# Background sums of the modulation: another set of rates at which weight tiles bring them along

## The chip, the cores and the metric

One core of one Trainium2 chip. The metric is the device time of one execution in microseconds, as the median of three runs. The engines are named as the profile names them: PE is TensorE, DVE VectorE, ACT ScalarE, POOL GpSimd, SP SyncE (which here issues the DMAs).

## The reference

A generator of two layers over 256 context tokens and 256 latent tokens, width 2048. Each layer modulates a normalised input with shift, scale and gate, which are products of a conditioning vector with a 2048 x 6144 matrix, then runs two attention groups and an output projection:

```
for l in range(DEPTH):                       # DEPTH = 2
    shift, scale, gate = split(silu(c) @ w_ada[l] + b_ada[l], 3)
    shift_c, scale_c, gate_c = split(silu(c_ctx) @ w_ada[l] + b_ada[l], 3)
    h_lat = rms_norm(x, norm_g[l]) * (1 + scale) + shift
    h_ctx = rms_norm(xc, norm_g[l]) * (1 + scale_c) + shift_c
    lat_a, lat_b = mixer_inputs(h_lat, w_in[l], ...)   # q, k, v, gate of GQA; low-rank q, kv, gate of latent attention
    ctx_a, ctx_b = mixer_inputs(h_ctx, w_in[l], ...)
    o_a = block_attention(GQA: latent queries over context and latent keys)
    o_b = block_attention(latent attention, likewise)
    x = x + gate * (concat(o_a * silu(g_gqa), o_b * silu(g_mla)) @ w_out[l])
    if l < DEPTH - 1:
        xc = xc + gate_c * (the same for the context tokens)
return rms_norm(x, final_g)
```

Scale and shift of layer 0 are wanted at once; the gates of layer 0 are wanted at its output projection, scale and shift of layer 1 at the start of layer 1, and the gate of layer 1 at its end.

## The kernel before

**Main work.** Every projection runs over weight tiles of 512 KB (288 KB where 288 columns remain). `wtile` (line 107) loads one on SP into one of four `raw` buffers, ACT rounds it to `hi` (line 116), and DVE, or POOL for every fifth tile, writes the remainder `lo` in two halves (line 118); `lo` has two buffers. `mm3` then makes each product of three matmuls (lines 143 to 145: hi by hi, lo by hi, hi by lo). In layer 0 a first part (until about 178 us) makes the first modulation and the first half of the input projection; then come the kv, q and gate projections with the two GQA head groups in between (`gqa_heads`, scores at line 605), the two low-rank projections `cq` and `ckv`, the four pairs of latent heads (`mla_qr`, line 691 for its rotary transposes, `mla_pair`, `mla_heads`), and the output projection in four column blocks c = 0 to 3 with residual update `go` and `xn` (lines 823 and 825). Layer 1 does the same for latent tokens alone, and its output projection is spread over its four head pairs.

**Background work.** What of the modulation is not wanted at once is computed on DVE beside this main work, by a generator `ada_rest` (line 308). One step of it (one turn of `ada_half`, line 263) loads one 512 KB piece of the transposed modulation matrix (`rad`, on SP, two buffers, issued behind the `raw` load before it) and multiplies it with the broadcast conditioning vectors `cb`, summing along the row: two sums of 512 elements for each vector (line 286, the output called `junk`, the sum `as`). The profile lists every sum as two DVE records, the sum itself and a short accumulator read. There are 128 steps: 96 with two vectors, so four sums each (gates of layer 0, then scale and shift of layer 1), and after these 32 with one vector, two sums each (gate of layer 1); 448 sums in all. `ada_done` stores each finished piece (`mod` tiles, `gate_d`).

**What sets when steps come.** Each weight tile adds the present rate to a debt, and takes one step for each whole unit of it:

```
self.bg_due += self.bg_rate
while self.bg and self.bg_due >= 1.0 and not self.hold:
    self.bg_due -= 1.0
    self.bg_step()
```

The rate is BG0 from line 937 on (the GQA part, the low-rank projections and their gates: 56 weight tiles), BG1 from line 972 on (latent attention of layer 0: 14 tiles), BG3 from line 997 on (output projection, c = 0 to 2: 24 tiles), then zero, and BG2 from line 1054 on in layer 1 (64 tiles). Behind c = 2 whatever of layer 1's scale and shift is missing is done at once (line 1013); in layer 1 what is still left after the first head pair is flushed (line 1105). The sums and their loads are put in with a lower priority (line 285, offset 1500), and a scheduler that simulates the timeline makes each engine's final order; so a step need not stand where its weight tile stands. Engines work in the order that results, each one strictly in turn.

Of the kernel before, what the change touches and what calls it, by code (L numbers as in the profile page):

```python
# [39 lines left out]

BG_LATER = 1500

BGS, BG0, BG1, BG3, BG2 = 5.0, 1.3, 1.1, 0.5, 0.4
TCKW = {"schedule_with_timeline_sim": True}


# [1168 lines left out]
```

## Time and profile before

| | us |
|---|---|
| median of three runs | 1396.11 (1395.94 to 1397.76) |
| the profiled execution | 1396.79 |
| its span, first to last instruction | 1395.0 |
| PE busy | 1326.7 (95%) |
| DVE busy | 1083.2 (78%) |
| ACT busy | 580.4 (42%) |
| POOL busy | 401.0 (29%) |
| mean granted clock of PE | 0.988 |

Stages by their start in the trace, in us: first part 0; kv and GQA of layer 0 178; the low-rank projections about 392; latent attention 462; output projection 692; layer 1 about 880; its latent attention about 1190.

Busy time counts records of instructions. A matmul's end is modelled, so a stall of PE is read from the list of waits and from the share of a stretch that PE is busy. In the windows an x counts records, and for line 286 two records are one sum.

### The profile page before, as it was taken

What the parts mean: (1) busy time and instruction counts of PE and PEld (TensorE: products, weight loads), DVE (VectorE), ACT (ScalarE), POOL (GpSimd) and SP (SyncE); (2) the same over time, 40 slices, a digit from 0 to 9 for tenths busy, and PEclk for the clock granted to TensorE, in tenths of its full rate; (3) what the DMA queues carried; (4) which work ended last, traced back from release to release, by engine and by line L of the source; (5) the groups of instructions that cost most, each with busy time, mean ns of one, the idle gap of its engine ahead of it and who ended that gap; (6) DMA issues with size and microseconds to landing.
All of it is one profiled execution on the core that took longest, in us unless ns stands there. A gap on an engine that the chain in (4) does not pass through costs nothing.

```text
span 1395.0 us, 20993 instructions
## 1 busy us (share of the span) xinstructions
PE 1326.7 (95%) x7516; PEld 1125.6 (81%) x7516; DVE 1083.2 (78%) x2297; ACT 580.4 (42%) x961; POOL 401.0 (29%) x385
## 2 busy tenths in 40 slices
PE   6999998998998999899999999999999999999996
PEld 5776786877887988788887888899888889889884
DVE  3776589999999989999985536976797676857566
ACT  4322213435342233354632224664554544454443
POOL 0110014523222230222222214442344231313335
PEclk9999999998999999999999999999999999999998
DMA  9997854554556666444475446565865647633444
GB/s 307 331 321 267 301 161 135 166 173 147 179 159 204 200 220 197 157 139 141 168 241 181 148 130 201 176 195 165 272 211 182 199 155 245 239 122 114 158 144 144
DMA packets 141128, 268.31 MB, mean 192 GB/s; under 512 B 8304, under 2 KB 53856, under 8 KB 139616
## 3 DMA queue, kind: packets, MB, share of 16 engines
q1 hardware_dynamic: 141024, 266.97, 59.4%
q8 instruction: 59, 0.97, 0.3%
q14 instruction: 45, 0.37, 0.1%
HBM read 260.61 MB, written 6.33 MB: 191 GB/s over the span
## 4 chain that ended last, share of the span: by engine, by line
PE 50%; DVE 28%; DMA 12%; issue 6%; ACT 2%; POOL 1%; SPq 1%; DVEq 0%; POOLq 0%; ACTq 0%
PE acc L143 14%; PE acc L145 14%; PE acc L144 14%; DVE junk L286 11%; DMA rad<-in_w_adaT 9%; DVE lo L118 7%; PE att L605 3%; PE att L240 2%; DVE sm L610 1%; PE att L628 1%; DMA raw<-in_w_in 1%; DMA ra<-in_w_ada 1%; DVE pt L150 1%; ACT hi L116 1%; DVE cb L466 1%
## 5 line engine op out<-in xcount | busy, mean ns | idle before, releaser
L116 ACT CAST hi<-raw 128x1024 fp32r<-128x1024 f32 (+2 forms) x279 | 272.2, 977 | 410.9 <-PE acc L144 202.0
L118 DVE TENSOR_TENSOR lo<-raw,hi 128x512 fp32r<-128x512 f32 (+2 forms) x446 | 306.1, 728 | 101.8 <-PE acc L145 42.1
L118 POOL TENSOR_TENSOR lo<-raw,hi 128x512 fp32r<-128x512 f32 (+2 forms) x112 | 151.1, 1369 | 469.6 <-PE acc L145 273.7
L143 PE MATMUL acc<-hi,h 128*128 128x512 f32 (+1 forms) x672 | 238.4, 359 | 10.2 <-DVE g L466 3.0
L144 PE MATMUL acc<-hi,h 128*128 128x512 f32 (+1 forms) x672 | 238.0, 357 | 0.0
L145 PE MATMUL acc<-lo,h 128*128 128x512 f32 (+1 forms) x672 | 225.5, 359 | 2.1 <-DVE lo L118 1.8
L286 DVE CUSTOM_DVE_ANT_0 junk<-rad,cb 128x512 bf16<-128x512 f32 x224 | 172.4, 770 | 68.1 <-DMA rad<-in_w_adaT 66.1
L286 DVE CUSTOM_DVE_ANT_0 junk<-rad,cb,as 128x512 bf16<-128x512 f32 x224 | 193.1, 862 | 3.3
L144 PE MATMUL acc<-h,lo 128*128 128x512 f32 (+1 forms) x512 | 170.9, 340 | 4.4 <-DVE lo L118 4.4
L145 PE MATMUL acc<-h,hi 128*128 128x512 f32 (+1 forms) x512 | 169.9, 338 | 0.0
L143 PE MATMUL acc<-h,hi 128*128 128x512 f32 (+1 forms) x512 | 163.7, 341 | 1.8 <-ACT hi L116 1.4
L616 POOL TENSOR_SCALAR p<-p,sm 128x512 f32<-128x512 f32 (+1 forms) x96 | 85.8, 899 | 270.2 <-DVE sm L614 226.0
L143 PEld LDWEIGHTS acc<-hi,h 128*128 128x128 f32 x672 | 126.6, 189 | 33.1 <-issue 11.5
L144 PE MATMUL acc<-hi,y 128*128 128x512 f32 x384 | 149.8, 391 | 0.2 <-DVE y L150 0.2
L143 PE MATMUL acc<-hi,y 128*128 128x512 f32 x384 | 149.0, 393 | 0.7 <-ACT y L149 0.7
L145 PE MATMUL acc<-lo,y 128*128 128x512 f32 x384 | 143.8, 394 | 3.0 <-DVE lo L118 2.0
L145 PEld LDWEIGHTS acc<-lo,h 128*128 128x128 f32 x672 | 124.5, 189 | 21.7 <-DVE lo L118 2.9
L144 PEld LDWEIGHTS acc<-hi,h 128*128 128x128 f32 x672 | 127.0, 189 | 15.8
L144 PEld LDWEIGHTS acc<-h,lo 128*128 128x128 f32 x512 | 96.8, 189 | 15.4 <-DVE lo L118 5.8
L143 PEld LDWEIGHTS acc<-h,hi 128*128 128x128 f32 x512 | 93.5, 190 | 14.7 <-issue 2.5
L145 PEld LDWEIGHTS acc<-h,hi 128*128 128x128 f32 x512 | 96.7, 190 | 9.7
L145 PEld LDWEIGHTS acc<-lo,y 128*128 128x128 f32 x384 | 72.0, 188 | 20.0 <-DVE lo L118 4.6
(218 smaller groups left out, 2253.5 us busy)
## 6 DMA issues: line engine op xcount, KB each, us to landing
rad<-in_w_adaT SPq DMA_DIRECT2D x128, 512.0 KB, 4.4
raw<-in_w_in SPq DMA_DIRECT2D x125, 512.0 KB, 4.4
raw<-in_w_out SPq DMA_DIRECT2D x72, 512.0 KB, 4.1
ra<-in_w_ada SPq DMA_DIRECT2D x32, 1024.0 KB, 9.1
raw<-in_w_in SPq DMA_DIRECT2D x48, 288.0 KB, 3.0
raw<-in_w_ukv SPq DMA_DIRECT2D x16, 512.0 KB, 3.6
raw<-in_w_uq SPq DMA_DIRECT2D x12, 512.0 KB, 3.7
xT<-in_xT SPq DMA_DIRECT2D x8, 512.0 KB, 7.6
```

The costliest lines, as they stand in the source:

```text
L116: nc.scalar.copy(h, t)
L118: e.tensor_tensor(out=lo[:, c], in0=t[:, c], in1=fr(h[:, c]), op=ALU.subtract)
L143: mm(out, lhsT=ah, rhs=bh, start=first, stop=False)
L144: mm(out, lhsT=al, rhs=bh, start=False, stop=False)
L145: return mm(out, lhsT=ah, rhs=bl, start=False, stop=last)
L150: self.nc.vector.tensor_tensor(out=lo, in0=src, in1=fr(hi), op=ALU.subtract)
L240: nc.tensor.matmul(ps[32 * g : 32 * g + 32, :], lhsT=self.scp[:, m + i, o : o + 32], rhs=rs[kind, m][:, i, :], start=run is runs[0] and j ...
L286: nc.vector.tensor_tensor_reduce(out=junk, in0=r[:, cs], in1=cb[:, v, cs], scale=1.0, scalar=o if i else 0.0, op0=ALU.mult, op1=ALU.add, a ...
L466: nc.vector.tensor_tensor(out=o, in0=ps, in1=o, op=ALU.add)
L605: self.order = nc.tensor.matmul(banks[j], lhsT=q[:, qs], rhs=k[:, ks], start=i == 0, stop=i == len(score) - 1)
L610: nc.vector.tensor_reduce(out=nb[:, c], in_=v, axis=AX.X, op=ALU.max)
L616: nc.gpsimd.tensor_scalar(out=pr[j], in0=pr[j], scalar1=l[:, j : j + 1], scalar2=1.0, op0=ALU.mult, op1=ALU.mult)
```

## The change

One line of numbers:

```
-BGS, BG0, BG1, BG3, BG2 = 5.0, 1.3, 1.1, 0.5, 0.4
+BGS, BG0, BG1, BG3, BG2 = 5.0, 1.0, 1.0, 1.5, 0.4
```

In the order of the code this is 56 steps instead of 72 or 73 at BG0, 14 instead of 15 at BG1, and 36 instead of 12 at BG3; 22 instead of 28 are left for layer 1. No instruction of the main work is added or taken away.

The order of DVE in layer 0's output projection, early in column block c = 1 (before: 763 to 779 us). `lo` is the remainder of a weight tile, `junk` and `as` a background sum; a row of `as` alone is the accumulator read; `mod` is a finished scale of layer 1. Before:

```order
L118 TENSOR_TENSOR lo_7492<-raw_7489,hi_7491 128x512 x2
L295 TENSOR_TENSOR as_4354<-as_4354,as_4355 128x32
L208 TENSOR_TENSOR mod_91<-as_4354,vec_90 128x32
L118 TENSOR_TENSOR lo_7533<-raw_7530,hi_7532 128x512 x2
L286 ISA junk_7679,as_7675<-rad_7677,cb_1649 128x512
L286 ISA as_7675 128x1
L286 ISA junk_7681,as_7675<-rad_7677,cb_1649,as_7675 128x512
L286 ISA as_7675 128x1
L118 TENSOR_TENSOR lo_7564<-raw_7561,hi_7563 128x512 x2
```

The same weight tiles after the change (`lo_7493` and `lo_7534` are the tiles that were `lo_7492` and `lo_7533`):

```order
L118 TENSOR_TENSOR lo_7493<-raw_7490,hi_7492 128x512 x2
L286 ISA junk_7503,as_4814<-rad_7497,cb_1649 128x512
L286 ISA as_4814 128x1
L286 ISA junk_7505,as_4814<-rad_7497,cb_1649,as_4814 128x512
L286 ISA as_4814 128x1
L286 ISA junk_7540,as_4814<-rad_7538,cb_1649 128x512
L286 ISA as_4814 128x1
L286 ISA junk_7542,as_4814<-rad_7538,cb_1649,as_4814 128x512
L286 ISA as_4814 128x1
L286 ISA junk_7544,as_4814<-rad_7538,cb_1649 128x512
L286 ISA as_4814 128x1
L118 TENSOR_TENSOR lo_7534<-raw_7531,hi_7533 128x512 x2
```

Where no sum or two stood between the remainders of two weight tiles, five or six stand now, and the finished scale comes some 25 us of the old time later.

The order of SP's loads in the same projection, column block c = 0 going over into c = 1. `raw` is a weight tile of the output projection, `rad` a piece of the modulation matrix. Before:

```order
L98 DMA rad_7352<-in_w_adaT 128x1024
L98 DMA raw_7386<-in_w_out 128x2x512
L98 DMA raw_7417<-in_w_out 128x2x512
L98 DMA rad_7424<-in_w_adaT 128x1024
L98 DMA raw_7458<-in_w_out 128x2x512
L98 DMA raw_7489<-in_w_out 128x2x512
L98 DMA rad_7496<-in_w_adaT 128x1024
```

After:

```order
L98 DMA rad_7262<-in_w_adaT 128x1024
L98 DMA raw_7306<-in_w_out 128x2x512
L98 DMA raw_7347<-in_w_out 128x2x512
L98 DMA rad_7272<-in_w_adaT 128x1024
L98 DMA raw_7398<-in_w_out 128x2x512
L98 DMA rad_7313<-in_w_adaT 128x1024
L98 DMA rad_7354<-in_w_adaT 128x1024
L98 DMA raw_7439<-in_w_out 128x2x512
L98 DMA rad_7364<-in_w_adaT 128x1024
```

One `rad` for two `raw` has become three for two, and a `raw` can now stand behind a `rad` that waits for its buffer.

The order of DVE in layer 1, when its latent attention begins (before: 1199 to 1206 us). `qr` is the rotated query part of latent attention, `kn` the keys of the first pair of heads. Before:

```order
L118 TENSOR_TENSOR lo_11965<-raw_11962,hi_11964 128x512 x2
L286 ISA junk_12285,as_7676<-rad_12283,cb_2829 128x512
L286 ISA as_7676 128x1
L694 TENSOR_TENSOR qr_11782<-att_11836,qr_11782 64x4x128
L286 ISA junk_12287,as_7676<-rad_12283,cb_2829,as_7676 128x512
L286 ISA as_7676 128x1
L150 TENSOR_TENSOR kn_11879<-acc_11889,kn_11879 128x512
L150 TENSOR_TENSOR kn_11879<-acc_11904,kn_11879 128x512
```

After:

```order
L118 TENSOR_TENSOR lo_11997<-raw_11994,hi_11996 128x512 x2
L694 TENSOR_TENSOR qr_11818<-att_11874,qr_11818 64x4x128
L150 TENSOR_TENSOR kn_11917<-acc_11927,kn_11917 128x512
L150 TENSOR_TENSOR kn_11917<-acc_11942,kn_11917 128x512
L694 TENSOR_TENSOR qr_11818<-att_11883,qr_11818 64x4x128
```

The sums that stood ahead of `qr` and `kn` are gone from this stretch.

Counted over the whole program, the sums stand so, by the old time of the main work around them (in us; the two orders were laid side by side by the instructions of the main work, which are the same):

| stretch | 250-305 | 305-332 | 332-346 | 346-430 | 430-462 | 462-600 | 600-700 | 700-745 | 745-825 | 825-1187 | 1187-1230 |
|---|---|---|---|---|---|---|---|---|---|---|---|
| sums before | 36 | 21 | 8 | 67 | 29 | 97 | 58 | 24 | 16 | 46 | 10 |
| sums after | 32 | 20 | 0 | 44 | 24 | 97 | 56 | 31 | 64 | 44 | 0 |

Within 430 to 462, between the `lo` that DVE wrote at 432 us and the next one that it wrote, at 444.5 us, stood twelve sums; eight stand there now.

## Rows read from the trace of the kernel before

**Rows 1.** Page: busy time and share by engine; then the chain that ended last.

```profile
PE 1326.7 (95%) x7516; PEld 1125.6 (81%) x7516; DVE 1083.2 (78%) x2297; ACT 580.4 (42%) x961; POOL 401.0 (29%) x385
...
PE 50%; DVE 28%; DMA 12%; issue 6%; ACT 2%; POOL 1%; SPq 1%; DVEq 0%; POOLq 0%; ACTq 0%
```

**Rows 2.** Page, groups: busy us, mean ns of one | idle before, releaser.

```profile
L286 DVE CUSTOM_DVE_ANT_0 junk<-rad,cb 128x512 bf16<-128x512 f32 x224 | 172.4, 770 | 68.1 <-DMA rad<-in_w_adaT 66.1
L286 DVE CUSTOM_DVE_ANT_0 junk<-rad,cb,as 128x512 bf16<-128x512 f32 x224 | 193.1, 862 | 3.3
```

**Rows 3.** Windows: length, PE, PEld, DVE, ACT, POOL busy (records), clock, DMA share, GB/s.

```profile
250.00:305.00 55.00, 55.00 (x282) 46.56 (x281) 54.72 (x127) 22.32 (x41) 22.28 (x19) 1.00 0.58 182
305.00:332.00 27.00, 19.22 (x102) 16.07 (x102) 26.61 (x74) 10.29 (x23) 11.25 (x16) 0.83 0.48 146
...
430.00:446.00 16.00, 14.06 (x63) 11.30 (x61) 14.71 (x35) 1.35 (x2) 3.18 (x2) 1.00 0.50 154
446.00:462.00 16.00, 12.50 (x90) 11.53 (x91) 15.86 (x36) 8.03 (x18) 10.92 (x12) 1.00 0.53 171
462.00:600.00 138.00, 130.48 (x748) 114.74 (x746) 127.99 (x306) 47.55 (x77) 28.73 (x28) 0.99 0.62 195
...
700.00:745.00 45.00, 43.67 (x223) 36.25 (x222) 35.48 (x87) 14.21 (x23) 9.81 (x9) 1.00 0.66 228
745.00:825.00 80.00, 80.00 (x354) 66.17 (x354) 35.07 (x66) 21.38 (x31) 18.37 (x14) 1.00 0.49 158
...
1187.00:1212.00 25.00, 22.31 (x128) 19.63 (x128) 23.20 (x38) 10.55 (x16) 9.62 (x6) 0.93 0.83 291
```

**Rows 4.** Windows of line 286 alone: length, DVE busy (records), clock, DMA share, GB/s.

```profile
745.00:825.00 80.00, 12.80 (x32) 1.00 0.49 158
825.00:1100.00 275.00, 28.48 (x56) 1.00 0.64 198
...
1187.00:1212.00 25.00, 9.08 (x16) 0.93 0.83 291
```

**Rows 5.** Waits of PE, 305 to 332: total us, times, longest.

```profile
PE att L145 <- DVE pt L150: 1.9, 2, 1.0
...
PE att L143 <- DVE g L636: 1.6, 1, 1.6
```

**Rows 6.** Waits of PE, 446 to 462.

```profile
PE acc L143 <- DVE cq L470: 2.8, 1, 2.8
PE att L535 <- POOL cq L566: 2.5, 3, 1.1
```

**Rows 7.** Chain of waits, 436 to 448: start us, us, what.

```profile
440.94 3.71 DMA rad<-in_w_adaT
```

**Rows 8.** Waits of PE, 1187 to 1212.

```profile
PE att L691 <- POOL tw L676: 1.0, 1, 1.0
PE acc L143 <- DVE kn L150: 1.0, 1, 1.0
PE att L605 <- ACT qr L693: 0.7, 1, 0.7
```

**Rows 9.** Chain of waits, 1196 to 1212.

```profile
1206.82 0.12 PE acc L144
...
1207.09 0.21 PE acc L143
...
1210.07 0.21 PE acc L145
```

**Rows 10.** Waits of DVE, 745 to 825.

```profile
DVE junk L286 <- DMA rad<-in_w_adaT: 19.4, 6, 5.6
DVE lo L118 <- PE acc L145: 12.1, 5, 4.3
```

**Rows 11.** Lines of DVE, 745 to 825: busy us, mean ns | idle before, releasers.

```profile
L118 DVE TENSOR_TENSOR lo<-raw,hi 128x512 fp32r<-128x512 f32 x24 | 17.1, 755 | 21.3 <-PE acc L145 12.1 <-issue 9.2
L823 DVE TENSOR_TENSOR go<-acc,gt 128x512 f32<-128x512 f32 x8 | 5.4, 686 | 3.0 <-ACT junk L332 1.4 <-POOL xn L825 1.4 <-PE acc L145 0.2
```

## The prediction

> **What bounds the kernel now.** I began with the busy shares and the chain that ended last [rows 1]. PE is busy for 1326.7 of 1395.0 us, so at most some 68 us are open to any reordering; yet the chain goes over DVE for 28% of the span and over DMA for 12%, which says that in some stretches PE follows DVE. The two groups of line 286 [rows 2] are the work that the change moves: 448 sums, (172.4 + 193.1) / 448 = 0.82 us each, and ahead of them DVE stood idle for 66.1 us until a `rad` landed. Then I read the windows stage by stage [rows 3] and asked in each which engine is short:
>
> - 250 to 305: DVE 54.72 of 55 us, PE 55.00. Both full, nothing lost.
> - 305 to 332, the end of the first GQA group: DVE 26.61 of 27, PE only 19.22, clock 0.83. PE is 7.8 us short and DVE is what it follows.
> - 430 to 462, the change from the query to the key and value low-rank projection: PE 14.06 of 16 and 12.50 of 16, 5.4 us short, DVE again nearly full.
> - 462 to 600: DVE 127.99 of 138, PE 130.48.
> - 700 to 825, output projection: PE 43.67 of 45 and 80.00 of 80; DVE 35.48 and 35.07.
> - 1187 to 1212, start of latent attention in layer 1: DVE 23.20 of 25, PE 22.31, clock 0.93.
>
> So the output projection is where PE is the bound and DVE has 44.9 of 80 us free, and the three other places are those where sums stand ahead of what PE waits for. That is the ground on which the change moves sums from the one kind of place to the other.
>
> **The change part by part.** The sums stay 448, with the same 128 loads; what counts is where they stand, by the table under the change. Each moved step takes its `rad` load along. The terms are against the profiled execution, 1396.79 us.
>
> *End of the first GQA group, 250 to 332.* Five sums fewer (4 + 1), 5 x 0.82 = 4.1 us of DVE work. Of the 7.8 us that PE lacks, 1.9 and 1.6 are waits for DVE itself, for the probabilities `pt` and the attention output `g` [rows 5]; the rest goes over ACT and POOL, or over the lower clock. In the new order one sum still stands between nearly every two DVE instructions of this stretch (21 become 20), so the waits stay mostly as they are, and only the backlog that DVE brings along shrinks. The eight sums at 332 to 346 go as well, and PE loses nothing there now. Ends 0 and -7.8; I take -2.0, about half of the 4.1, nearer to zero, since the order at the stall itself hardly changes.
>
> *346 to 430.* 23 sums fewer, but the list of waits has none of PE here: 0.
>
> *Low-rank projections, 430 to 462.* PE waits 2.8 us for the eviction of `cq` and then three times, 2.5 in all, for POOL on the same `cq` [rows 6]. On DVE, twelve sums stand ahead of the `lo` of 444.5 us, and the one right before it waited 3.71 us for its `rad` [rows 7]; with it `lo` and the eviction behind it waited. Now eight stand there: four fewer are 3.3 us at 0.82, more than the 2.8. The POOL waits are a chain behind the eviction and stay. Ends 0 and -5.3; I take -2.5, the greater part of the first wait.
>
> *462 to 700.* 97 sums stay 97 and 58 become 56: the debt that the old rates had run up was worked off before, and the scheduler fills this stretch up again. 0. So the relief is confined to the front, about 41 sums by 475 us.
>
> *Output projection, 700 to 745.* Seven sums more, 5.7 us at 0.82, onto a DVE that is busy 35.48 of 45 us [rows 3]. It has room, but PE loses 1.3 us here already. Ends 0 and +3; I take +0.5.
>
> *Output projection, 745 to 825.* PE does 354 matmuls here [rows 3], 24 for a weight tile, so 14.75 tiles, one in 5.4 us. DVE now carries 64 sums instead of 16. Their price here is 12.80 / 16 = 0.80 [rows 4], so 51.2; `lo` and `go` add 17.1 + 5.4 [rows 11]: 73.7 of 80 us, 92%. That still fits, but it is no longer free: before, DVE waited up to 4.3 us for PE to free a `lo` buffer, 12.1 us in five waits [rows 10], and that margin is what the sums now eat. Five or six sums between two `lo` take 4.0 to 4.8 us, with 1.4 for `lo` itself 5.4 to 6.2, against 5.4. POOL takes every fifth `lo`, which gives the time back. Loads: the rate adds one step for a tile, about 15 loads of 0.52 MB, 98 GB/s on top of 158, so 256, under the 291 GB/s that one stretch moved [rows 3]. They must land in turn with two buffers, and a `rad` was what DVE waited for here even before, 19.4 us in six waits, at no cost to PE [rows 10]. A wait for a `rad` would now hold `lo` behind it on DVE and a `raw` behind it on SP, and PE waits for both. Ends 0 and +8 (next part); I take +1.5, near zero, because a density of the same kind in 250 to 305 left PE at 55.00 of 55 [rows 3].
>
> The price of a sum is not the same everywhere: 28.48 / 28 = 1.02 us in 825 to 1100 and 9.08 / 8 = 1.14 in 1187 to 1212, against 0.80 in the output projection [rows 4]. POOL is busy 9.62 of 25 us in the dear stretch, 18.37 of 80 in the cheap one [rows 3]. The Trainium skill, page "SBUF — State Buffer", section "Who interferes with whom", speaks against the change with that: a DVE instruction with two inputs in SBUF contends with a GpSimd instruction that reads SBUF, since its second input comes through a shared port that is locked exclusively. The rows agree in direction. By it all work put beside the residual update of POOL would run at the dearer price, which is the second rival below.
>
> *Layer 1, 1187 to 1230.* The ten sums here go altogether, 8 x 1.14 = 9.1 us of DVE in the first 25 us. PE waits three times, 1.0 + 1.0 + 0.7 = 2.7 us [rows 8], for `tw`, `kn` and `qr`; sums stand directly ahead of `qr` and `kn`. Behind these waits the matmuls of 256 columns follow one another 0.21 us apart instead of 0.12 for 15 matmuls [rows 9]: the granted clock is at its lower level, 1.4 us more. Without the sums `kn` and `qr` come earlier and that stretch probably stays at the full clock. The wait for `tw` is on POOL and may stay. Ends 0 and -4.1; I take -3.0. The flush behind the first head pair has nothing left to do.
>
> Sum: -2.0 - 2.5 + 0.5 + 1.5 - 3.0 = -5.5, so 1391.3 for the profiled execution. The median of before lies 0.7 under its profiled one, so 1390.6.
>
> **Rivals.**
>
> *Nothing measurable.* The waits named have other ends than the sums: PE waits for ACT and POOL in chains that are as long without them, the scheduler keeps 97 sums in 462 to 600 and 20 at 305 to 332, and one or two us come back at the output projection. For: the order at the greatest loss hardly changes. Against: at `cq` and in layer 1 the sums stand in the order right ahead of what PE waits for. Reliefs of -0.5, -1, -1 with +1 to +2 in the output projection: 1395 to 1396.
>
> *Slower: DVE becomes the bound in the output projection.* 22.5 us for `lo` and `go` leave 57.5 for 64 sums: from 0.90 us a sum on, PE follows DVE. At the 1.02 of the stretch 825 to 1100 it is 65.3 + 22.5 = 87.8 us, 7.8 more than the 80, and late `rad` landings come on top in the same way. For: the new order puts sums right beside the `go` and `xn` updates, and the margin is 8%. Against: the price read in this very stretch is 0.80. With half of the relief (-3.7) it is about 1400.
>
> *More: the end of the first GQA group gives way.* If DVE's backlog at 305 is what starts the stall and the lower clock, 7.8 us go at once and not 2.0: about 1385. For: DVE is full from 250 on. Against: 20 of 21 sums stay there.
>
> *The change does not do what it says:* it says evenly over the layer, but 462 to 700 is unchanged. If the relief in 430 to 462 also fails to reach PE because the sums only stand in a longer row later, only layer 1 is left, -3.0 + 2.0: 1395, a case of the first rival.
>
> **How the numbers follow.** A measurement here tells about 0.2%, 2.8 us, from no change. My forecast, 1390.6 with 1388 to 1393 of its own: 0.46. More, 1385: 0.10. Nothing measurable, 1393.3 to 1398.9: 0.28. Slower, 1399 to 1403: 0.16. Faster is the first two, 0.56. The range leaves out the far half of the second and of the last: 1385.5 to 1399.5.
>
> **What the profile after would show.** PE in 430 to 446 at more than 15 of 16 us and no wait of 2.8 for `cq`; in layer 1 no wait for `kn` or `qr` and clock 1.00 over that stretch; in the output projection DVE at some 90%, line 286 at some 51 us for 64 sums and PE still at 98% or more. I am wrong if PE waits there for `lo` more than 3 us in all (the sum's price or the `rad` landing would say which), or if 305 to 332 has changed by more than 3 us either way, since I hold its order to be nearly the same.

## The result, and the profile after

The changed kernel takes 1410.78 us (median of four runs, 1406.60 to 1415.52) against 1396.93 us for the kernel before (median of four as well): a ratio of 1.0106, 95% interval 1.0083 to 1.0128. It is slower by 14 us, outside the predicted range, where a gain of 5.5 was forecast. The profiled execution took 1412.46 us, its span 1410.7.

Page of the changed kernel, to be held against [rows 1, 2]: busy time and share by engine, the chain that ended last, and the two groups of background sums (busy us, mean ns of one | idle before).

```profile
PE 1331.1 (94%) x7516; PEld 1125.3 (80%) x7516; DVE 1084.1 (77%) x2297; ACT 578.9 (41%) x959; POOL 403.5 (29%) x385
...
PE 52%; DVE 24%; DMA 15%; issue 5%; POOL 2%; ACT 1%; SPq 1%; DVEq 0%; POOLq 0%; ACTq 0%
...
L286 DVE CUSTOM_DVE_ANT_0 junk<-rad,cb 128x512 bf16<-128x512 f32 x224 | 173.9, 776 | 82.9 <-DMA rad<-in_w_adaT 80.6
...
L286 DVE CUSTOM_DVE_ANT_0 junk<-rad,cb,as 128x512 bf16<-128x512 f32 x224 | 183.9, 821 | 3.5
```

DVE does the same work in the same time. What grew is the time it stands still for a `rad`: 80.6 us instead of 66.1, and in the chain DMA went from 12% to 15% of the span. All of that growth stands in the front (12.7 to 36.1 us, under e9 to e13 below); from 676 to 862 us DVE waits as long for `rad` as before.

The stages show where the time went. Windows of the changed kernel (length, PE, PEld, DVE, ACT, POOL busy with records, clock, DMA share, GB/s), beside [rows 3]; the first is the end of the first GQA group, the third the end of column block c = 0, the fourth the rest of c = 1 and 2:

```profile
305.00:337.00 32.00, 22.25 (x120) 19.00 (x119) 29.40 (x77) 11.24 (x25) 14.97 (x18) 0.89 0.36 111
...
705.00:755.00 50.00, 49.85 (x256) 41.79 (x254) 41.50 (x105) 15.84 (x29) 7.93 (x10) 1.00 0.66 230
755.00:775.00 20.00, 16.23 (x64) 12.31 (x63) 19.21 (x34) 5.83 (x11) 9.98 (x6) 0.94 0.59 166
775.00:862.00 87.00, 81.78 (x349) 66.06 (x348) 62.52 (x138) 20.83 (x30) 17.85 (x13) 0.98 0.67 213
```

The output projection, where PE was busy 80.00 of 80 us before, now has 3.8 us without PE in one stretch of 20 and 5.2 in the next 87. And the first GQA group ends no better: PE lacks 9.8 us there, before 7.8.

To put a price on each stage I laid the executions side by side by PE's progress. The main work is the same in all kernels, so I summed the matmuls' usual start-to-start times in their order and read, for each kernel, when it had done the same amount. What a kernel loses against the kernel before between two such points is that stage's cost. This table goes through the whole study (one profiled execution each, in us, minus is a gain; the last column is the difference at the end). The stages are named by the old time: front 191 to 674 (kv, GQA, low-rank projections, latent attention), start of the output projection 674 to 694, c = 0 694 to 756, its change to c = 1 756 to 776, c = 1 and 2 776 to 836, c = 3 and first half of layer 1 836 to 1041, second half to 1217. What lies before 191 us, where the rates play next to no part, came out from -0.4 to +3.1 (changed kernel +2.6), so the last column carries up to 3 us that no stage explains.

| kernel | front | start | c = 0 | change 0 to 1 | c = 1, 2 | to 1041 | to 1217 | end |
|---|---|---|---|---|---|---|---|---|
| changed | +2.3 | +5.6 | -0.4 | +5.2 | +7.9 | +1.2 | -8.9 | +15.7 |
| e1 old front, 1.5 in output projection | -1.4 | +0.4 | +2.9 | +5.3 | +11.0 | -1.5 | -14.5 | +3.8 |
| e2 old rates, layer 1 sooner | +0.8 | +0.8 | -0.7 | 0.0 | 0.0 | +4.3 | -6.0 | -0.4 |
| e3 changed, no update on POOL | +4.1 | +6.3 | -2.1 | 0.0 | +11.3 | -1.3 | -5.5 | +13.6 |
| e4 changed, no loads there | +3.2 | +1.5 | +0.7 | +6.2 | +5.2 | +1.4 | -8.9 | +12.3 |
| e5 changed, neither | +1.1 | +1.5 | -0.3 | 0.0 | 0.0 | +0.1 | -8.4 | -3.3 |
| e6 changed, three `rad` | -2.2 | +5.7 | -0.4 | +5.3 | +2.0 | +1.1 | -7.9 | +4.9 |
| e7 as e1, update on DVE | -1.2 | +1.2 | +0.7 | 0.0 | +10.7 | -1.2 | -14.4 | -3.4 |
| e8 as e7, three `rad` | -1.1 | +0.5 | +1.2 | 0.0 | +5.4 | -0.3 | -14.4 | -6.5 |
| e9 changed, nothing in the front | -36.8 | +6.7 | -0.4 | +5.3 | +7.1 | -0.6 | -7.7 | -25.3 |
| e10 changed, no loads in the front | -7.8 | +6.6 | -0.4 | +5.3 | +8.1 | +1.2 | -9.7 | +6.4 |
| e11 old rates, update on DVE, three `rad` | -0.7 | +1.2 | -1.4 | 0.0 | 0.0 | -0.1 | +1.1 | +0.9 |
| e12 as e8, 1.1 in output projection | +4.3 | +0.9 | +0.9 | 0.0 | +0.6 | +1.3 | -13.0 | -4.3 |
| e13 old rates, no loads in the front | -5.8 | +1.0 | -0.6 | 0.0 | 0.0 | -0.2 | -3.4 | -6.5 |
| e14 changed, update on DVE, three `rad` | -2.2 | +6.9 | -0.9 | 0.0 | +0.8 | -0.7 | -9.3 | -5.8 |

The changed kernel, e3, e4 and e5 have DVE's order in the front in common, for all or most of it, and read +1.1 to +4.1, so a front entry is good to about 1.5 us in most executions. Not in all: e8, e11 and e12 share DVE's order up to 672 us and read -1.1, -0.7 and +4.3 (the execution of e12 is the slowest of its nine). The stages of the output projection repeat within about 1 (changed, e9, e10).

So the change loses 18.3 us between 674 and 836 (5.6 - 0.4 + 5.2 + 7.9), gains 8.9 in layer 1, and gets no relief in the front.

At the change from c = 0 to c = 1 the trace shows what happens on DVE, here a part of its timeline in the changed kernel (start us, us, instruction):

```profile
755.70 2.38 DVE L118 TENSOR_TENSOR lo<-raw,hi 128x512 fp32r<-128x512 f32 x2
...
759.21 0.73 DVE L286 CUSTOM_DVE_ANT_0 junk<-rad,cb,as 128x512 bf16<-128x512 f32 x1
...
759.98 1.66 DVE L286 CUSTOM_DVE_ANT_0 junk<-rad,cb 128x512 bf16<-128x512 f32 x1
...
761.57 0.68 DVE L823 TENSOR_TENSOR go<-acc,gt 128x512 f32<-128x512 f32 x1
762.18 0.74 DVE L286 CUSTOM_DVE_ANT_0 junk<-rad,cb,as 128x512 bf16<-128x512 f32 x1
...
762.96 1.66 DVE L286 CUSTOM_DVE_ANT_0 junk<-rad,cb 128x512 bf16<-128x512 f32 x1
...
769.15 1.63 DVE L286 CUSTOM_DVE_ANT_0 junk<-rad,cb,as 128x512 bf16<-128x512 f32 x1
...
770.72 2.34 DVE L118 TENSOR_TENSOR lo<-raw,hi 128x512 fp32r<-128x512 f32 x2
```

POOL at the same time (the same columns, idle time before in brackets), and PE behind it:

```profile
759.36 1.73 POOL L825 TENSOR_TENSOR xn<-xn,go 128x512 f32<-128x512 f32 x1 [2.45 <-DVE go L823]
762.34 1.73 POOL L825 TENSOR_TENSOR xn<-xn,go 128x512 f32<-128x512 f32 x1 [1.24 <-DVE go L823]
```

```profile
772.51 0.80 PE L145 MATMUL acc<-lo,y 128*128 128x512 f32 x1 [3.35 <-DVE lo L118]
773.10 0.63 PE L143 MATMUL acc<-hi,y 128*128 128x512 f32 x1
773.52 0.63 PE L144 MATMUL acc<-hi,y 128*128 128x512 f32 x1
...
776.25 0.39 PE L145 MATMUL acc<-lo,y 128*128 128x512 f32 x1
776.48 0.39 PE L143 MATMUL acc<-hi,y 128*128 128x512 f32 x1
```

A sum that starts while an update of `xn` runs takes 1.66 us; with no POOL work beside it, it takes 0.69 or 0.74. The sum at 759.21 was under way when the update at 759.36 began: it took 0.73, and the update 1.73 instead of the 1.28 to 1.30 that it takes alone. The pair `lo` at 755.70, beside an update, takes 2.38 instead of 1.29. The pair of the next tile and the sum ahead of it, beside a `lo` that POOL writes from 768.84 on, take 2.34 and 1.63. Three sums beside updates and the first pair are 4.0 us longer than alone, the last sum and the second pair 1.9: 5.9 us on DVE, where the stage loses 5.2. DVE alternates `go`, sum, sum, and the `lo` that PE needs stands behind all of it: PE waits 3.35 us, and then its matmuls start 0.42 us apart instead of 0.23 for six matmuls; over 772.5 to 775.1 us the granted clock is 0.50, the lower of its two levels.

At the start of the output projection the other kind is seen. Chain of waits of the changed kernel, 684 to 697:

```profile
683.54 0.96 ACT hi L116
684.50 0.15 SPq L98
...
684.70 5.96 DMA rad<-in_w_adaT
...
690.79 1.30 DVE junk L286
...
692.14 1.64 DVE junk L286
```

SP stood at a `raw` until ACT had read the buffer; the `rad` behind it was issued only then and landed 5.96 us later. DVE, with the scores of the last heads behind that sum, stood still for the last 3.10 us of it.

### The profile page after: what moved, and what is told of

Its sections match the earlier page's. It is cut to its first block, busy times and chain, and to the rows that moved or that the text cites. A ratio compares the mean times of both kernels' runs of the same rounds, so it can differ in the third digit from the quotient of the medians.

```text
span 1410.7 us, 20995 instructions
## 1 busy us (share of the span) xinstructions
PE 1331.1 (94%) x7516; PEld 1125.3 (80%) x7516; DVE 1084.1 (77%) x2297; ACT 578.9 (41%) x959; POOL 403.5 (29%) x385
## 4 chain that ended last, share of the span: by engine, by line
PE 52%; DVE 24%; DMA 15%; issue 5%; POOL 2%; ACT 1%; SPq 1%; DVEq 0%; POOLq 0%; ACTq 0%
PE acc L145 14%; PE acc L144 14%; PE acc L143 14%; DMA rad<-in_w_adaT 12%; DVE junk L286 10%; DVE lo L118 6%; PE att L605 3%; DMA ra<-in_w_ada 2%; PE att L240 2%; PE att L628 2%; DVE sm L610 1%; DMA xT<-in_xT 1%; PE att L143 1%; PE att L145 1%; PE att L144 1%
## 5 line engine op out<-in xcount | busy, mean ns | idle before, releaser
L286 DVE CUSTOM_DVE_ANT_0 junk<-rad,cb 128x512 bf16<-128x512 f32 x224 | 173.9, 776 | 82.9 <-DMA rad<-in_w_adaT 80.6
L286 DVE CUSTOM_DVE_ANT_0 junk<-rad,cb,as 128x512 bf16<-128x512 f32 x224 | 183.9, 821 | 3.5
L145 PE MATMUL acc<-lo,y 128*128 128x512 f32 x384 | 146.6, 401 | 10.7 <-DVE lo L118 9.4
L143 PE MATMUL acc<-hi,y 128*128 128x512 f32 x384 | 151.0, 397 | 3.6 <-ACT y L149 1.5
L144 PE MATMUL acc<-hi,y 128*128 128x512 f32 x384 | 151.6, 396 | 1.3 <-DVE y L150 1.3
L144 PEld LDWEIGHTS acc<-hi,h 128*128 128x128 f32 x672 | 126.5, 188 | 15.7
```

The source lines that it names most:

```text
L143: mm(out, lhsT=ah, rhs=bh, start=first, stop=False)
L144: mm(out, lhsT=al, rhs=bh, start=False, stop=False)
L145: return mm(out, lhsT=ah, rhs=bl, start=False, stop=last)
L286: nc.vector.tensor_tensor_reduce(out=junk, in0=r[:, cs], in1=cb[:, v, cs], scale=1.0, scalar=o if i else 0.0, op0=ALU.mult, op1=ALU.add, a ...
```

## The experiments

e1 to e4, e5 to e8, e9 to e12, and e13 and e14 ran on four different chips, each beside the kernel before (1396.47, 1395.80, 1394.57 and 1394.59 us there), so between these groups ratios compare better than times. The scheduler lays the sums anew in each kernel; where that matters it is said.

### e1: the output projection's rate alone

```
-BGS, BG0, BG1, BG3, BG2 = 5.0, 1.0, 1.0, 1.5, 0.4
+BGS, BG0, BG1, BG3, BG2 = 5.0, 1.3, 1.1, 1.5, 0.4
```

> Old rates 1.3 and 1.1, only the output projection's rate raised to 1.5. The order up to 700 us is that of the kernel before; 55 sums stand in 745 to 825 instead of 16, and none is left for 1100 on. Theory A, the output projection costs by itself what the trace of the change shows there (+18 us between 676 and 836 us of the old time, and some 7 us given back in layer 1): 1405 to 1410 us, with no loss before 676. Theory B, the loss comes from the thinner front (loads of the modulation that come late there): within 3 us of the kernel before, less the 7 given back in layer 1.

Measured 1401.88 us against 1396.47 for the kernel before, ratio 1.0051 (1.0031 to 1.0071). The front, whose order is the old one, is within 1.4 us of before; the output projection loses 19.6 us (0.4 + 2.9 + 5.3 + 11.0), layer 1 gains 14.5. Theory A holds for the place, though the total is lower than its range, since I had put the gain of layer 1 at 7. The cost sits in the raised rate.

### e2: layer 1 sooner

```
-BGS, BG0, BG1, BG3, BG2 = 5.0, 1.0, 1.0, 1.5, 0.4
+BGS, BG0, BG1, BG3, BG2 = 5.0, 1.3, 1.1, 0.5, 0.6
```

> All rates of the kernel before, only layer 1's raised from 0.4 to 0.6, so that the ten sums in 1187 to 1230 stand earlier in layer 1 (28 become 40 in 825 to 1100). If those ten sums cost what the prediction took for them: 3 us less than before, up to 8 by the trace of the change. If that gain came from elsewhere in the changed order: within 1 us of before.

Measured 1400.79 us, ratio 1.0026 (1.0012 to 1.0040): slower, which neither expectation had. The profiled execution is the shortest of its ten, 1396.37, so what made the others slower does not show in the table. It shows -6.0 us where the ten sums went away, as wanted, and +4.3 where they now stand. By this one execution layer 1 pays about as much for them in either place, and only sums that leave layer 1 are a gain.

### e3: no update on POOL

```
-                e.tensor_tensor(out=xc, in0=xc, in1=o, op=ALU.add)
+                if l == 1 or c == 3:
+                    e.tensor_tensor(out=xc, in0=xc, in1=o, op=ALU.add)
```

> The changed kernel without the residual update on POOL in column blocks 0 to 2 of layer 0 (the addition of go to xn is left out; go itself stays). The sums beside it then have no POOL instruction next to them. Theory A1, contention of sums and update sets lo back at the two changes of column block: the waits for lo there (3.5 and 2.0 us) and the slow matmuls behind them go, 5 to 10 us less than the changed kernel. Theory A2, the sums' loads are late: under 2 us less.

Measured 1410.55 us. As a total that fits A2: hardly less than the changed kernel. But by stages it splits. At the change from c = 0 to c = 1 the 5.2 us go altogether. Window of the same stretch without the update:

```profile
744.00:768.00 24.00, 24.00 (x110) 19.74 (x109) 21.11 (x52) 7.59 (x14) 0.65 (x1) 1.00 0.74 255
```

PE is full there, with 18 sums on DVE. Not all of it is the price: between the first `go` and the `lo` that PE had waited for stand 9 sums here, 11 in the changed kernel. In c = 1 and 2 the loss is 11.3 instead of 7.9: by its timeline the sums arrive there with `rad` after `rad` late, and `lo` after them (PE waits at 840). Waits of PE for `lo` and of DVE for `rad`, 700 to 862:

```profile
PE acc L145 <- DVE lo L118: 4.7, 1, 4.7
```

```profile
DVE junk L286 <- DMA rad<-in_w_adaT: 15.7, 15, 2.7
```

Two causes, each of which gets its way where the other is gone.

### e4: no loads in the output projection

```
-                r = self.raw(self.a["w_adaT"][...], 1, 1024, "rad")[1][:, 0, :]
+                if self.bg_rate == BG3:
+                    r = self.radk
+                else:
+                    r = self.raw(self.a["w_adaT"][...], 1, 1024, "rad")[1][:, 0, :]
...
+        self.radk = self.cp.tile([P, 1024], F32, name="radk", tag="radk")
+        nc.sync.dma_start(out=self.radk, in_=a["w_adaT"][0:P, 0:1024])
```

> The changed kernel, but the sums of the steps that the output projection takes read one piece of the modulation matrix that stays in SBUF, so these steps load nothing (their sums are of the wrong rows). Theory A2, late loads hold lo: the waits in column block 2 (2.8 us at 841) and at the start of the output projection go, 6 to 12 us less than the changed kernel, and raw loads no longer stand behind rad. Theory A1, contention and a full DVE: under 3 us less, the waits at the changes of column block stay.

Measured 1408.00 us, ratio 1.0080 against 1.0106 for the changed kernel: about 3 us less, not the 6 to 12 of theory A2. The start of the projection falls from 5.6 to 1.5, c = 1 and 2 from 7.9 to 5.2; the change from 0 to 1 stays, at 6.2. (Without loads the scheduler also lays some ten of the sums of 745 to 825 sooner, in e4 as in e5.) Window of that change:

```profile
750.00:774.00 24.00, 20.22 (x77) 15.01 (x77) 23.61 (x46) 5.90 (x11) 9.62 (x6) 0.90 0.31 100
```

DVE full, PE 3.8 us short, clock 0.90, and the DMA queues nearly idle: here it is not the loads.

### e5: neither

> The changed kernel without the update of xn on POOL in column blocks 0 to 2 and with sums there that load nothing (both edits of the two runs before together). If the loss between 676 and 836 us of the old time is these two causes and nothing else, it is under 5 us there instead of 18, and the kernel ends 15 us sooner than the changed one, near 1396. If the mere number of sums on DVE is a third cause, 8 us or more stay there.

Both edits together, one execution: 1393.73 us. The output projection from 674 to 836 is +1.2 us, and no stage behind its start loses anything. A window of that stretch, and waits of DVE, 676 to 850:

```profile
735.00:840.00 105.00, 103.93 (x467) 85.58 (x466) 81.55 (x191) 29.20 (x45) 10.38 (x8) 1.00 0.41 130
```

```profile
DVE lo L118 <- PE acc L145: 18.7, 4, 9.6
```

DVE carries its sums (53.53 us for 70 of them in this window by the rows of `junk`) and still waits for PE to give `lo` buffers back, 18.7 us in four waits. The number of sums is no third cause, as far as this order tells; e14 below settles it with the changed kernel's number of sums and all loads. The arithmetic of the prediction, that 64 sums fit into the room, was right, and what it left out decided.

### e6: three buffers for the modulation's pieces

```
-NB_BLK, NB_RAW, NB_HI, NB_LO, NB_RAD = 14, 4, 3, 2, 2
+NB_BLK, NB_RAW, NB_HI, NB_LO, NB_RAD = 14, 4, 3, 2, 3
```

> The changed kernel with three buffers for the modulation's pieces instead of two. If loads that come late are what took the relief in the front (26 us of waits for rad on DVE in 250 to 470, before 3.6) and held lo at the start and the end of the raised rate: 4 to 9 us less than the changed kernel, waits for rad in the front under half. If a rad is late since it stands on SP behind a raw that waits for its own buffer, a third buffer does little: under 2 us.

Measured 1401.43 us, ratio 1.0035 (1.0012 to 1.0058): 9 us less than the changed kernel, the upper end of the first expectation. It comes in c = 1 and 2 (2.0 instead of 7.9; the waits of DVE for `rad` from 676 to 862 fall from 20.3 us to 7.4) and in the front (-2.2 instead of +2.3). The start of the projection stays at 5.7, where the late `rad` had stood behind a `raw`, and so does the change from 0 to 1, 5.3. The waits for `rad` in the front did not halve (below), so that part of the expectation failed.

### e7 and e8: the update on DVE, and three buffers too

```
-                e = nc.vector if l == 1 and c == 3 else nc.gpsimd
+                e = nc.vector if l == 1 and c == 3 or l == 0 and c < 3 else nc.gpsimd
```

with the rates of e1; e8 has NB_RAD = 3 besides.

> Rates 1.3, 1.1, 1.5, 0.4 (old front, raised output projection, as in the first run of this study) with the update of xn in column blocks 0 to 2 on DVE instead of POOL: 12 instructions of about 0.7 us more for DVE, and no sum slowed next to an update. If contention is the cause at the changes of column block: about 8 us less than that first run, 1393 to 1396. If DVE's own load is: the 2.8 us more of each block come on top, 1402 or more.

> The run before with three rad buffers. If late loads hold lo at the end of the raised rate as well: 3 to 5 us less than the run before, below the kernel before the change by up to 8. If not, the same as the run before.

e7 measured 1395.33 us, ratio 0.9998 (0.9976 to 1.0021), 6.5 less than e1, and the change from 0 to 1 costs nothing: with the update among its own instructions DVE has 12 more to do and is done sooner. The sums stand in the same places (3 of 98 moved). Not all of it is the price of a sum: between the first `go` and the `lo` that PE needs, DVE's waits for `rad` fell too, from 4.9 us to 1.4. c = 1 and 2 stay as they were, 10.7 against 11.0. e8 measured 1390.60 us, ratio 0.9957 (0.9938 to 0.9976): c = 1 and 2 halve, to 5.4. This kernel beats the kernel before, by 0.4%.

### e9, e10 and e13: what the front pays for sums and for loads

e9 leaves the front's steps out, sums and loads (and sets their results to zero):

```
+                if self.bg_rate == BG0:
+                    yield
+                    continue
                 r = self.raw(self.a["w_adaT"][...], 1, 1024, "rad")[1][:, 0, :]
```

e10 and e13 have the edit of e4 with the condition on the front rates instead, e13 with all rates as before the change.

> The changed kernel with the steps at the front rates (the 70 weight tiles of GQA, the low-rank projections and latent attention of layer 0) left out, sums and loads. What the front loses to the background in all: against the kernel before, 191 to 674 us of the old time becomes shorter by what the sums cost PE there. By the prediction, whose front stalls are DVE's: 10 us or more shorter. If those stalls are chains of scores, ACT and POOL that stand without sums too: under 5 us.

> The changed kernel with the same sums in the front, but on one piece of the modulation matrix that stays in SBUF (sums of the wrong rows), so that no sum there waits for a load. If late loads took the relief, 191 to 674 us of the old time is 4 us or more shorter than in the changed kernel, with the sums still there. If not: within 2 us of the changed kernel.

> All rates of the kernel before, its front sums (191 to 674 us) on one piece of the modulation matrix that stays in SBUF. It belongs beside the run that did so with the changed rates, which gained 10 us there. If late loads are what ate the relief of the lower rates, the front gains little here, under 4 us, and is longer than that run's by 4 us or more, the relief that the prediction took. If loads cost the old rates as much (8 us or more gained), the lower rates bring the front nothing even without loads.

e9, one execution, 1371.52 us: the front is 36.8 us shorter. Its windows at the places where PE was short:

```profile
300.00:320.00 20.00, 20.00 (x110) 17.05 (x108) 12.22 (x23) 10.97 (x18) 8.21 (x12) 1.00 0.43 128
...
400.00:450.00 50.00, 50.00 (x300) 45.51 (x299) 14.82 (x27) 14.28 (x25) 12.72 (x17) 1.00 0.28 78
```

PE is full and its clock whole. All those stalls, the ones for ACT and POOL included, come from the background work, its sums or its loads. The first rival, chains that are as long without the sums, is out.

e10 (1403.30 us, one execution) has the sums of the changed front without their loads: -7.8, which is 10.1 less than the changed kernel. e13 (1390.21 us, one execution) has the old front's sums without loads: -5.8. So doing without loads is worth 10 us to the changed front and 6 to the old one. Waits of DVE for `rad` between 190 and 676 us (total us, times, longest), of the kernel before, of the changed one, and of e6, which has three buffers:

```profile
DVE junk L286 <- DMA rad<-in_w_adaT: 12.7, 13, 1.8
```

```profile
DVE junk L286 <- DMA rad<-in_w_adaT: 36.1, 28, 5.1
```

```profile
DVE junk L286 <- DMA rad<-in_w_adaT: 28.8, 16, 4.5
```

Without loads the changed rates' front is 2.0 us shorter than the old ones' (-7.8 against -5.8); with loads, it loses 4.3 more to them (10.1 - 5.8), and +2.3 remains. The expectation had wanted 4 us of relief and under 4 of loads at the old rates: right in direction, neither in size, and a difference of 2.0 is less than two executions can tell. Nor do the sums stand in place: without loads the scheduler lays them sooner, in e10 some 69 in 346 to 430 instead of 44, and 84 in 462 to 600 instead of 100. What the lower rates bring by themselves is not shown.

### e11, e12 and e14: which part makes the better kernel

All three have the update on DVE and three `rad` buffers. Rates: e11 as before the change, e12 1.3, 1.1, 1.1, 0.4, and e14 those of the change.

> All rates of the kernel before, with the update of xn on DVE in column blocks 0 to 2 and three rad buffers. It tells whether the gain of the best kernel so far comes from these two edits alone or from the rates together with them. From the rates with them: within 2 us of the kernel before. From the edits alone: 4 us or more less.

> Rates 1.3, 1.1, 1.1, 0.4, update on DVE, three rad buffers: 35 sums in 745 to 825 instead of 55, and 28 in layer 1 before 1100 instead of 8. If the dose in the output projection still costs (6.5 us of loss there at 55 sums): 2 to 5 us less than that kernel, near 1387. If layer 1 asks as much for the 20 sums that move there: the same, 1390 to 1392.

> The changed rates with the update of xn on DVE in column blocks 0 to 2 and three rad buffers. If contention with the update and late loads are what made the change slow, the whole loss goes: 1388 to 1394. If the lower front rates cost something of their own: 1396 or more, above the 1390.6 of the old front rates with the same two edits.

e11: 1397.51 us, ratio 1.0017 (0.9998 to 1.0037). The two edits alone bring nothing. e12: 1389.77 us, ratio 0.9959 (0.9946 to 0.9972), the same as e8; the loss in c = 1 and 2 is down to 0.6, and layer 1 gives 1.4 less. e14: 1392.24 us, ratio 0.9974 (0.9953 to 0.9995): the very rates that were 14 us slower gain 0.26% once the update is off POOL and a third buffer is there. That closes the account of the output projection with all its sums and loads in place: the change from 0 to 1 costs 0.0, c = 1 and 2 cost 0.8, and what stays is the start, +6.9.

## Why the prediction was wrong

**Output projection: +2.0 forecast, +18.3 found.** The step that failed is "73.7 of 80 us, 92%. That still fits". The sum itself was sound: over 775 to 862 the sums take 41.28 us over 104 records, 0.79 each, against the 0.80 forecast, and e5 and e14 show that they fit. But the bound was never the average. The prediction had the local figure too, 5.4 to 6.2 us from one `lo` to the next against 5.4, and let POOL's share of `lo` give the time back. The price of a sum is 0.69 or 0.74 next to no POOL work and 1.66 when it starts beside the update, and the updates, all four of a column block, fall into the few us in which DVE also has four `go` and the first `lo` of the next block to do. Windows of line 286 alone in the changed kernel, the 20 us around that change and the 87 us behind:

```profile
755.00:775.00 20.00, 13.21 (x26) 0.94 0.59 166
775.00:862.00 87.00, 41.28 (x104) 0.98 0.67 213
```

13 sums at 1.02 us, and DVE 19.21 of 20 us busy. The rival "DVE becomes the bound" named this mechanism with a threshold of 0.90 us; it was tested against the mean of the whole stretch instead of the stretch where POOL is busy, and got 0.16. The sign of being wrong that the prediction had set, PE waiting for `lo` for more than 3 us in all, came. Waits of PE, 675 to 865 of the changed kernel (before, from 676 to 862: 0.4 us):

```profile
PE acc L145 <- DVE lo L118: 8.2, 5, 3.4
```

The Trainium skill, page "SBUF — State Buffer", section "Who interferes with whom", has that a DVE instruction with two inputs in SBUF contends with a GpSimd instruction that reads SBUF; the trace agrees, 1.66 against 0.74 us for the sum and 1.73 against 1.3 for the update.

Then the loads. "I take +1.5, near zero" rested on the density of 250 to 305, where PE lost nothing. It does not carry over: a `rad` here goes behind a `raw` on SP, and a `raw` waits for ACT and `lo`, so DVE waits for `rad`, `lo` behind it, `raw` behind that, and the delays can feed each other (the chain at 684 shows the first half; the second is argued). What changed is not how long DVE waits for `rad` but what it has left besides. Waits of DVE, 676 to 862 us, before and after:

```profile
DVE junk L286 <- DMA rad<-in_w_adaT: 20.9, 8, 5.6
DVE lo L118 <- PE acc L145: 17.6, 7, 4.3
```

```profile
DVE junk L286 <- DMA rad<-in_w_adaT: 20.3, 12, 3.4
...
DVE lo L118 <- PE acc L145: 2.3, 3, 1.3
```

The margin that the prediction named is used up, and each late `rad` now comes through to `lo`. The prediction wrote this chain down and gave it no price of its own. e3 and e5 give one: 11.3 us in c = 1 and 2 with the update gone, none with the loads gone too. The stage 674 to 694 lies in 462 to 700, which the prediction put at 0 since the number of sums hardly changes; e4 and e5 (1.5 without loads) point to the loads for its 5.6 us. Why that place pays in every kernel with the changed front and two or three buffers and not with the old front (0.4 to 1.2) is not settled: the order of loads there differs, and I tried no run for it.

**Front: -4.5 forecast, +2.3 found.** By parts: the first GQA group, -2.0 forecast, was the wrong sign, and 278 to 433 us lost 8.1, about half of it in 346 to 430, which had been put at 0. (305 to 332 itself changed by +1.0, within the 3 us that the prediction had allowed.) PE waits, 250 to 345, of the changed kernel, beside [rows 5]:

```profile
PE att L143 <- DVE sm L614: 5.0, 1, 5.0
PE att L628 <- POOL p L616: 3.9, 3, 1.7
```

The low-rank projections were right in mechanism and taken too small: the wait for `cq` [rows 6] is gone, of 2.5 us on POOL, which the prediction had staying, 1.3 stay, and 433 to 460 gained 4.7 in the changed kernel and 4.5 to 5.0 in e3 to e6; -2.5 forecast.

```profile
PE att L535 <- POOL cq L566: 1.3, 3, 0.5
```

The step that failed is the bound "Ends 0 and -7.8": it let in no loss, and gave no reason for that beyond fewer sums. [rows 2] had 66.1 us of DVE standing still for `rad`, about as much as the 68 us in which PE is not busy at all, and I priced sums and never those waits. Fewer sums did not mean shorter waits: from 190 to 676 us they rose from 12.7 to 36.1 us. SP's own waits, 250 to 470, before and after, tell what held the loads (`as` gives a `rad` buffer back, `lo` a `raw` buffer):

```profile
SPq L98 <- DVE as L286: 98.4, 30, 7.9
SPq L98 <- DVE lo L118: 53.4, 23, 4.3
```

```profile
SPq L98 <- DVE lo L118: 110.9, 23, 10.5
SPq L98 <- DVE as L286: 29.8, 10, 7.9
```

Before, SP mostly stood at a `rad` whose buffer was not yet free, so each was issued as early as it could be. Now it stands mostly at a `raw`, for up to 10.5 us, and a `rad` behind it is issued late and waited for. That the third buffer helps the changed front (e6 and e14 -2.2, against +1.1 to +4.1 with two) fits; that this chain is the whole of the loss is not shown. Nor is it known how far the lower rates help at all: without loads 2.0 us, with three buffers -2.2 (e14) against -1.1, -0.7 and +4.3 for the old rates (e8, e11, e12), all within what an execution can scatter.

**Layer 1: -3.0 forecast, -8.9 found.** Mechanism right, size off: the term counted three waits and a slow stretch at 1187 to 1212 [rows 8, 9] and no more. Window of the same place after:

```profile
1192.00:1232.00 40.00, 39.90 (x278) 37.18 (x277) 27.60 (x47) 18.47 (x25) 11.48 (x8) 1.00 0.66 223
```

PE is full there, clock 1.00, and the old 1192 to 1217 alone gives 5.0 us by the same reckoning as in the table, more than the bound of 4.1; it is the same 5.0 in every run but e11 and e13, the two in which the ten sums stand there still. The other 3.9 come between 1041 and 1192, where the new order has nearly as many sums as the old one. The runs with the same number of sums in layer 1 (e3 to e6, e9, e10, e14) read -0.4 to -4.6 there, so some of it is scatter of single executions; the rest is open. e1, e7 and e8, with 8 sums behind 825 us instead of 56, gain 14.4 or 14.5 in the same stage. Layer 1 is a dear place for a sum, and I had priced only its one visible stall.

**462 to 700, 0 forecast:** it held from 462 to 674 (+0.7), by the same reckoning as in the table, and failed in the 20 us behind (+5.6), where the number of sums stayed and the order of the loads did not.

**The rivals.** "Nothing measurable" and "more" are out. "Slower" was the outcome, and 1410.78 lies far above its 1399 to 1403: it had 7.8 us for the output projection, where 18.3 came. Its dearer price alone made 11.4 (e4, the change from 0 to 1 with c = 1 and 2, without loads), and of the late loads, on top "in the same way", it gave no number.

## What to carry to other kernels

Background work on an in-order engine is paid where something urgent stands behind it in the queue, so ask of each stretch of some ten us, and not of the stage's average, what comes next on that engine, and what POOL does beside it meanwhile (here a sum became 1.66 us long instead of 0.74). A background step is a load as much as an instruction: price the wait for its load with everything queued behind it, on the engine and on the DMA queue. Here the move of sums was +14 us as made, and -2 us (0.26%) with the update taken off POOL and one more load buffer; with the old front rates besides it was -5 (e8, e12), while those two edits alone changed nothing.

## What the runs showed of the hardware

Moving an addition from an engine with time to spare (POOL, 29% busy) onto a full one (DVE, 19.21 of 20 us busy in the changed kernel's stretch) made the full one faster. e6 and e14 differ in that alone, and at the change from c = 0 to c = 1 their first `go` starts at the same time, 748.14 us. Rows of DVE in e6, then in e14:

```profile
753.70 1.65 DVE L286 CUSTOM_DVE_ANT_0 junk<-rad,cb 128x512 bf16<-128x512 f32 x1
...
764.43 2.34 DVE L118 TENSOR_TENSOR lo<-raw,hi 128x512 fp32r<-128x512 f32 x2
```

```profile
753.11 0.69 DVE L825 TENSOR_TENSOR xn<-xn,go 128x512 f32<-128x512 f32 x1
753.71 0.68 DVE L286 CUSTOM_DVE_ANT_0 junk<-rad,cb 128x512 bf16<-128x512 f32 x1
...
760.66 1.29 DVE L118 TENSOR_TENSOR lo<-raw,hi 128x512 fp32r<-128x512 f32 x2 [0.49 <-PE acc L145]
```

An update on DVE is about as long as a sum, and the sums beside it keep their 0.7 us. The first nine sums behind that `go` are done at 761.30 in e6 and at 760.16 in e14, with four updates more among them. The `lo` that PE needs gains more, 3.8 us, since in e14 nine sums stand ahead of it and in e6 eleven; PE's loss there goes from 5.3 us to 0.0.

A wait of PE of 3.35 us was followed by 2.6 us of matmuls at the lower granted clock, 0.42 us apart instead of 0.23: about a third again on top of the wait.
